# A hybrid streaming layer: TensorE in text order through attention, nine query products moved across the border between the kinds of heads, and an output half begun in score banks

## The chip, the cores and the metric

The kernel runs on one core of a Trainium2 chip. The metric is device time in microseconds (us) of one launch; the kernel before takes 1536.96 us (median of three runs, 1535.45 to 1539.69).

## The reference

One layer over 1072 rows: 32 sample rows (they also see a cache of 512 past rows), 16 learned meta rows and 1024 prompt rows, width 1024.

- RMSNorm, then one input projection into a query latent (384), a key/value latent (256), a shared rotary key (32), and query, key, value of eight "FoX" heads of 64, with a log forget value for each head.
- Heads 0 to 7 (latent heads): query from the normalised query latent (64 plain and 32 rotary columns each), key and value from the key/value latent; a mask by chunks of 64 rows.
- Heads 8 to 15 (FoX heads): causal, with the difference of cumulated log forget values added to the logits.
- Softmax, times value; both groups concatenated, one output projection (1024 x 1024), residual.
- RMSNorm, SwiGLU feed-forward (width 2816), residual, final RMSNorm.

All of it is float32: each operand is held as a rounded high part and a low part, and a product is three matmuls (high x high, high x low, low x high).

## The kernel before, in words

**Stages.** Input projection (to some 233 us of the span), attention head by head (to some 689 us), then the part called C: second half of the output projection and the feed-forward (to the end). Heads run in the order 8 to 15, then 0 to 7.

**One head.** The rows are nine query tiles (`QT`, L37): tile 0 of 48 rows, tiles 1 to 8 of 128. `attention` (L725) takes the tiles in two groups, first (5, 6, 7, 8), then (1, 2, 3, 4) with (0). For each tile, `scores` (L560) multiplies query by key into a score buffer `psS` (two buffers of two PSUM banks; tile 8 also takes one of the two `psT` banks), DVE finds the row maximum (L592) and ACT does the exponential (L597). Between the scores the loop steps a generator `state["pend"]`: the value work (`values`, L619) of the group before. A step transposes one block of probabilities on TensorE into a `psT` bank (L651, L627), ACT and DVE split it (L67, L68), and the value matmuls (L667, L668, L665, L637) of the block two steps back (`LAG`) are issued into the single bank `po`. When a group's last value matmul is done, `out` copies half of `po` on ACT (L675) and adds the halves on DVE (L678); only then may the next group write `po`. After each second head, `finish_pair` (L684) adds three steps that divide by the row sums (L706 on TensorE, L712, L713, L715).

**Fillers.** After each score tile and each step, `fill()` may draw from a second generator; it draws `rate` units a call. During heads 8 to 15 it is `latent_heads` (L445): 16 key products, 26 value products, then 18 query products (six weight blocks in the order 4, 5, 0, 1, 2, 3, three column chunks each; blocks 4 and 5 are the rotary parts). The query products read the query latent, which is loaded (L61, tiles `A_hi`, `A_lo`) into the memory that the key/value latent leaves. Their results pass through a ring of six small buffers (`room`) on their way to DRAM. At head 15 the loop empties this filler, and then `masks()` loads the shared mask operand B3 (tile `room`, from `sKR` and `sM`) into two places of the same ring; the third matmul of each score of heads 0 to 7 reads B3 (`psS<-room,x`). In heads 0 to 7 the filler is `out_half` (L537): 24 products of the FoX half of the output projection, in two half products each, with tile `psF`.

**What sets the order.** The framework's scheduler orders each engine's instructions, TensorE's too, by the text's order and by its own forecast of when operands are ready. On the chip each queue then runs in that order. SyncE (SP) issues all loads, GpSimd (POOL) the stores to DRAM.

**Border to part C.** After the last head the remaining value steps are run. The pools of attention close, and part C opens `psG` (six banks) for its products. It takes the output products of the latent half (`units`, L835) in groups of four, k = 0 to 2 of all four first and then k = 3, since the pair of heads 6 and 7 is row 3 of `A_hi` and `A_lo`; the matmuls are L845 to L847.

Of the kernel before, what the change touches and what calls it, by code (L numbers as in the profile page):

```python
# [9 lines left out]
F32 = mybir.dt.float32  # L10
# [32 lines left out]
RING = 6  # L43
# [6 lines left out]
def trunk(ctx: ExitStack, tc: tile.TileContext, a):  # L50
# [392 lines left out]
    mixed = {}  # L443

    def latent_heads():  # L445
# [24 lines left out]
        ws = [weights(*todo[0])]  # L470
        yield
        for m in range(6):
            if m + 1 < 6:
                ws.append(weights(*todo[m + 1]))
            w = ws[m]
            if m < 4:
                for c0, n in KC:
                    ps = psF.tile([128, 512], F32, tag="psF", name="psF")
                    mm3(ps[:, :n], lambda k: w[0][:, k], lambda k: w[1][:, k],
                        lambda k: l_hi[:, k, c0:c0 + n], lambda k: l_lo[:, k, c0:c0 + n], 2)  # L480
                    spill(es, sK[m, :, :, c0:c0 + n], ps[:, :n], n)
                    yield
            else:
                for k0, n in [(128 * i, 128) for i in range(4)] + [(PAST + t0, n) for t0, n in QT]:
                    ps = psF.tile([128, 512], F32, tag="psF", name="psF")
                    for k in range(2):
                        s_hi, s_lo = l_hi[:, k, k0:k0 + 128], l_lo[:, k, k0:k0 + 128]
                        pe.matmul(ps[:, :256], s_hi, w[0][:, k], start=(k == 0), stop=False)
                        pe.matmul(ps[:, :256], s_hi, w[1][:, k], start=False, stop=False)
                        pe.matmul(ps[:, :256], s_lo, w[0][:, k], start=False, stop=(k == 1))  # L490
                    spill_v(None, k0, 4 * (m - 4), ps[:n, :256], n, part()[:, :512].rearrange("p (h d) -> p h d", h=4))
                    yield
# [9 lines left out]
        ws = [weights("w_uq", order[0], 3, 128)]  # L502
        yield
        for i, m in enumerate(order):
            if i + 1 < 6:
                ws.append(weights("w_uq", order[i + 1], 3, 128))
            w = ws[i]
            for cs, (c0, n) in zip(trig, CC):
                ps = psF.tile([128, 512], F32, tag="psF", name="psF")
# [4 lines left out]
                else:  # L514
# [8 lines left out]
                    if turn[0] == RING:  # L523
                        turn[0] = 3
                yield

# [10 lines left out]
    def out_half():  # L537
# [4 lines left out]
        for m in range(8):  # L542
            out_weights(m + 2)
            w = w_ring[m]
            for c0, n in CC:
# [4 lines left out]
                for k in range(4):  # L550
# [3 lines left out]
                    if k == 1:  # L554
                        yield
                dve.tensor_tensor(out=xt[:, :n], in0=ps[:, :n], in1=xt[:, :n], op=ALU.add)
                put(sX2[128 * m:128 * m + 128, c0:c0 + n], xt[:, :n])
                yield

# [162 lines left out]

    state = {"pend": iter(()), "n": 0}

    def attention(hs, filler, steps, last):  # L725
        rate, owed = steps / (25.0 * (len(hs) - 0.7)), [0.0]

        def fill():
            if last and h == hs[0] and grps[0][0] == 5:
                return  # L730
            owed[0] += rate
            while owed[0] >= 1:
                next(filler, None)
                owed[0] -= 1

        rs = raw = None
        for h in hs:
# [14 lines left out]
            for grps in (((5, 6, 7, 8),), ((1, 2, 3, 4), (0,))):  # L752
                todo = [i for g in grps for i in g]
                P, done = {}, 0
                for j, i in enumerate(todo):
# [15 lines left out]
                state["pend"] = chain(*gens)  # L771
        for _ in filler:
            pass

# [11 lines left out]

    attention(range(8, 16), latent_heads(), 62, False)
    mixed["A"] = (slot("A_hi"), slot("A_lo"))

    attention(range(0, 8), out_half(), 48, True)  # L790
    for _ in state["pend"]:
        pass
    B.close()
    hpx.close()


    with ExitStack() as C:
# [34 lines left out]
        big = [tuple(rows4(t) for t in mixed[g]) for g in ("A", "B")]  # L832
        m_hi, m_lo = big[0]
        W = None
        units = [(m, c) for m in range(8) for c in FC]  # L835
        for u0 in range(0, len(units), 4):
            part = []
            for m, (c0, n) in units[u0:u0 + 4]:
                out_weights(8 + m + 2)
                part.append((m, c0, n, psG.tile([128, 512], F32, tag="psG", name="psG"), w_ring[8 + m]))  # L840

            for ks in ((0, 1, 2), (3,)):
                for m, c0, n, ps, w in part:
                    for k in ks:
                        pe.matmul(ps[:, :n], w[0][:, k], m_hi[:, k, c0:c0 + n], start=(k == 0), stop=False)  # L845
                        pe.matmul(ps[:, :n], w[0][:, k], m_lo[:, k, c0:c0 + n], start=False, stop=False)
                        pe.matmul(ps[:, :n], w[1][:, k], m_hi[:, k, c0:c0 + n], start=False, stop=(k == 3))  # L847
            if u0 == 12:
# [16 lines left out]
        def gate_up(W, c0, n, ah, al, between=None):  # L865
# [3 lines left out]
            def product(j):  # L869
                ps = psG.tile([128, 512], F32, tag="psG", name="psG")  # L870
                marks[2] = mm3(ps[:, :n], lambda k: gh[:, j, k], lambda k: gl[:, j, k], lambda k: big[k // 4][0][:, k % 4, cs], lambda k: big[k // 4][1][:, k % 4, cs], 8)
                return ps
# [20 lines left out]
        def down(parts, c0, n, norm=False, then=None):  # L893
            cs = slice(c0, c0 + n)
            for m in range(8):
                ps = psG.tile([128, 512], F32, tag="psG", name="psD")
                down_mm(ps[:, :n], m, cs, parts, True, True)
# [25 lines left out]
        def down_final(prev, cur, c0, n):  # L923

            cs = slice(c0, c0 + n)
            pairs = [psG.tile([128, 512], F32, tag="psG", name="psD").rearrange("p (a b) -> p a b", a=2) for _ in range(4)]
            for part in (prev, cur):
# [161 lines left out]
```

## Time and profile before

| | us |
|---|---|
| Median of three runs | 1536.96 |
| Profiled execution, its time | 1537.25 |
| Its span, first to last instruction | 1535.5 |
| TensorE (PE) busy | 1493.0 |
| VectorE (DVE) busy | 971.5 |
| ScalarE (ACT) busy | 591.4 |

PE is TensorE's matmuls, PEld its weight loads, which run beside the matmuls. A busy PE is not PE at its peak, since a matmul's shown duration covers the pipeline too. Granted clock is the share of TensorE's full clock that the chip gave. Between the span and the time of the execution lie 1.75 us.

### The profile page before, as it was taken

The numbers are of one execution on the slowest core, as the hardware profiler recorded it, in microseconds if no ns is written. First come the engines' busy times: TensorE is split into PE (matmuls) and PEld (weight loads), VectorE is DVE, ScalarE is ACT, GpSimd is POOL, SyncE is SP. The second block draws the span as 40 slices with busy tenths as digits, with TensorE's granted clock in tenths as the row PEclk, the third lists the DMA queues.
The fourth block names the chain that finished last, engine by engine and source line by source line (L and its number), as shares of the span: only waits on it lengthen the run. The fifth ranks groups of instructions, "written<-read, shape, count | busy, mean of one in ns | idle before, by whom it ended". The sixth has DMA issues, their size and how long they took to land.

```text
span 1535.5 us, 24295 instructions
## 1 busy us (share of the span) xinstructions
PE 1493.0 (97%) x9317; PEld 1433.5 (93%) x9317; DVE 971.5 (63%) x1861; ACT 591.4 (39%) x1198; POOL 198.5 (13%) x331
## 2 busy tenths in 40 slices
PE   9999998999898999989999999999999999999996
PEld 8999997888787898979999999999999999999996
DVE  8874626787966776766855655555555555655547
ACT  7443436777655666654511111111111121111124
POOL 0343242422131211200000000000000000000001
PEclk9999999999999999999999999999999999999999
DMA  6689567778587686515111111111111111111003
GB/s 196 233 258 299 172 210 249 238 218 262 147 238 185 174 212 161 148 41 206 34 50 44 54 42 42 42 42 42 42 42 42 53 58 53 44 42 42 28 1 115
DMA packets 87636, 184.19 MB, mean 120 GB/s; under 512 B 9754, under 2 KB 52954, under 8 KB 87428
## 3 DMA queue, kind: packets, MB, share of 16 engines
q1 hardware_dynamic: 70592, 128.34, 28.8%
q0 software_dynamic: 16928, 54.29, 10.1%
q8 instruction: 74, 1.21, 0.3%
q14 instruction: 42, 0.34, 0.1%
HBM read 123.93 MB, written 58.67 MB: 119 GB/s over the span
## 4 chain that ended last, share of the span: by engine, by line
PE 88%; DVE 4%; ACT 3%; issue 2%; DMA 1%; POOL 1%; DVEq 0%; SPq 0%; POOLq 0%; ACTq 0%
PE psG L122 11%; PE psG L121 11%; PE psG L123 11%; PE psD L890 5%; PE psD L891 5%; PE psD L889 5%; PE psS L589 5%; PE psT L651 4%; PE psA L123 3%; PE psA L121 3%; PE psA L122 3%; PE po L667 2%; PE po L668 2%; PE psA L386 1%; PE psA L387 1%
## 5 line engine op out<-in xcount | busy, mean ns | idle before, releaser
L898 DVE TENSOR_TENSOR x<-psD,x 128x408 f32<-128x408 f32 (+1 forms) x496 | 236.2, 522 | 4.3 <-PE psD L891 4.3
L122 PE MATMUL psG<-B_lo,gh 128*128 128x408 f32 (+1 forms) x528 | 172.8, 327 | 0.0
L121 PE MATMUL psG<-B_hi,gh 128*128 128x408 f32 (+1 forms) x528 | 172.8, 327 | 0.0
L122 PE MATMUL psG<-A_lo,gh 128*128 128x408 f32 (+1 forms) x528 | 172.6, 327 | 0.0
L121 PE MATMUL psG<-A_hi,gh 128*128 128x408 f32 (+1 forms) x528 | 172.3, 326 | 0.0
L891 PE MATMUL psD<-ah,dl 128*128 128x408 f32 (+1 forms) x528 | 172.1, 326 | 0.0
L123 PE MATMUL psG<-B_hi,gl 128*128 128x408 f32 (+1 forms) x528 | 171.8, 325 | 0.0
L123 PE MATMUL psG<-A_hi,gl 128*128 128x408 f32 (+1 forms) x528 | 171.8, 325 | 0.0
L890 PE MATMUL psD<-al,dh 128*128 128x408 f32 (+1 forms) x528 | 171.7, 325 | 0.0
L889 PE MATMUL psD<-ah,dh 128*128 128x408 f32 (+1 forms) x528 | 170.9, 325 | 0.5 <-ACT ah L67 0.5
L878 ACT ACTIVATE sl<-sl 128x408 f32<-128x408 f32 (+1 forms) x66 | 33.1, 503 | 351.3 <-DVE sl L877 351.2
L882 DVE TENSOR_TENSOR sq<-psG,rb 128x408 f32<-128x408 f32 (+1 forms) x66 | 35.0, 530 | 156.5 <-PE psG L123 156.5
L68 DVE TENSOR_TENSOR ptl<-psT,pth 128x512 fp32r<-128x512 f32 x192 | 104.6, 552 | 28.7 <-ACT pth L67 26.6
L592 DVE TENSOR_REDUCE nm<-psS 128x1 f32<-128x656 f32 (+2 forms) x144 | 104.0, 724 | 27.2 <-PE psS L589 25.6
L67 ACT ACTIVATE pth<-psT 128x512 fp32r<-128x512 f32 (+4 forms) x208 | 99.2, 480 | 55.7 <-PE psT L651 46.5
L830 POOL TENSOR_TENSOR acc<-acc,sq 128x408 f32<-128x408 f32 x10 | 10.8, 1076 | 812.4 <-ACT sq L829 811.9
L877 DVE TENSOR_TENSOR sl<-psG,rb 128x408 f32<-128x408 f32 (+1 forms) x66 | 34.9, 530 | 123.0 <-PE psG L123 123.0
L67 ACT ACTIVATE ah<-sl 128x408 fp32r<-128x408 f32 (+1 forms) x66 | 33.2, 503 | 197.2 <-DVE sl L883 125.8
L589 PE MATMUL psS<-b,a 128*128 128x328 f32 (+4 forms) x360 | 99.9, 331 | 7.4 <-ACT pb L597 6.1
L889 PEld LDWEIGHTS psD<-ah,dh 128*128 128x128 f32 x528 | 99.2, 188 | 0.9 <-ACT ah L67 0.7
L122 PEld LDWEIGHTS psG<-B_lo,gh 128*128 128x128 f32 x528 | 99.2, 188 | 0.5 <-issue 0.3
L121 PEld LDWEIGHTS psG<-B_hi,gh 128*128 128x128 f32 x528 | 99.2, 188 | 0.5 <-issue 0.2
(274 smaller groups left out, 3803.5 us busy)
## 6 DMA issues: line engine op xcount, KB each, us to landing
sg<-w_gu SPq DMA_DIRECT2D x44, 512.0 KB
a<-sQ SPq DMA_DIRECT2D x56, 268.0 KB
b<-sK SPq DMA_DIRECT2D x32, 396.0 KB
sg<-w_down SPq DMA_DIRECT2D x22, 512.0 KB
v<-sV SPq DMA_DIRECT2D x16, 512.0 KB
wst<-w_in SPq DMA_DIRECT2D x13, 512.0 KB
sV<-vt POOLq DMA_DIRECT2D x24, 256.0 KB, 4.5
sK<-room POOLq DMA_DIRECT2D x14, 396.0 KB, 4.9
```

The costliest lines, as they stand in the source:

```text
L67: first = act.activation(hi, src, AF.Copy)
L68: return first.ins, eng.tensor_tensor(out=lo, in0=src, in1=f32(hi), op=ALU.subtract).ins
L121: pe.matmul(ps, whi(k), rhi(k), start=(k == 0), stop=False)
L122: pe.matmul(ps, whi(k), rlo(k), start=False, stop=False)
L123: last = pe.matmul(ps, wlo(k), rhi(k), start=False, stop=(k == K - 1))
L589: pe.matmul(out, qa[:K, t0:t0 + nq], kb[:K, k0 + c:k0 + c + w], start=(j == 0), stop=last)
L592: dve.tensor_reduce(out=nm[:nq, j:j + 1], in_=src, axis=AX.XY if len(src.shape) == 3 else AX.X, op=ALU.max, negate=True)
L651: pe.transpose(out=pt[:, 128 * g:128 * g + 128], in_=tiles[g][1][:, c:c + 128], identity=ident)
L889: pe.matmul(ps, dh[:, m], ah[:, cs], start=first and j == 0, stop=False)
L890: pe.matmul(ps, dh[:, m], al[:, cs], start=False, stop=False)
L891: pe.matmul(ps, dl[:, m], ah[:, cs], start=False, stop=last and j == len(parts) - 1)
L898: dve.tensor_tensor(out=x2[:, m, cs], in0=ps[:, :n], in1=x2[:, m, cs], op=ALU.add)
```

## The change

- The score buffers `psS` outlive attention.
- From head 8 to the end of attention TensorE runs in the order of the text (`tc.manual_schedule`); the other engines are still ordered by the scheduler.
- `latent_heads` yields the units that a draw costs. Before the query products it idles three draws in place of one, and the query latent is loaded in three chunks of columns. After nine query products (blocks 4, 5, 0) it marks `keys`; from there on its results keep off the two ring places of B3, so `masks()` can load B3 at head 15's start. The nine products of blocks 1, 2, 3 are drawn at 0.25 a call in head 15 and in the first group of head 0; what is left of them is drawn before head 1's second group.
- `out_half` follows in the same chain of fillers. Rates change from 62 and 48 steps over 7.3 heads to 59 over 7.3 and 50 over 7.75.
- `begin()` runs k = 0 to 2 of the first four output products of the latent half, into the four banks of two score buffers, one step of three matmuls after each of the nine value steps left, and three steps behind them.
- Part C uses these four banks and two of `psG` in rotation (`bank()`), in place of six of `psG`.

```diff
-    psS = B.enter_context(tc.tile_pool(name="psS", bufs=2, space=PSUM))
+    psS = ctx.enter_context(tc.tile_pool(name="psS", bufs=2, space=PSUM))
...
             turn[0] = (turn[0] + 1) % (RING + 1)
+            if state["keys"] and turn[0] in (RING - 2, RING - 1):
+                turn[0] = RING
...
-        move(c_hi, sCQ[:, :, 0].rearrange("k p t -> p k t"))
-        move(c_lo, sCQ[:, :, 1].rearrange("k p t -> p k t"))
+        for c0, n in CC:
+            for j, t in enumerate((c_hi, c_lo)):
+                move(t[:, :, c0:c0 + n], sCQ[:, :, j, c0:c0 + n].rearrange("k p t -> p k t"))
...
-        yield
+
+        for _ in range(3):
+            yield 1
         for i, m in enumerate(order):
...
+            if i == 3:
+
+                state["keys"] = True
+                yield 0
...
+        state["made"] = True
+        yield 0
...
-        rate, owed = steps / (25.0 * (len(hs) - 0.7)), [0.0]
+        rate, owed = steps / (25.0 * (len(hs) - (0.25 if last else 0.7))), [0.0]
         def fill():
-            if last and h == hs[0] and grps[0][0] == 5:
-                return
-            owed[0] += rate
+
+            border = h == 15 or (last and h == hs[0] and len(grps) == 1)
+            owed[0] += 0.25 if border else rate
             while owed[0] >= 1:
-                next(filler, None)
-                owed[0] -= 1
+                if last and border and state["made"]:
+                    return
+                owed[0] -= next(filler, 1)
...
-            if h == hs[-1]:
-                for _ in filler:
-                    pass
-                if not last:
-                    masks()
+            if h == hs[-1] and not last:
+                while not state["keys"]:
+                    next(filler)
+                masks()
...
+                if last and h == hs[1] and len(grps) == 2:
+                    while not state["made"]:
+                        next(filler)
+                    mixed["A"] = (slot("A_hi"), slot("A_lo"))
...
-    attention(range(8, 16), latent_heads(), 62, False)
-    mixed["A"] = (slot("A_hi"), slot("A_lo"))
-
-    attention(range(0, 8), out_half(), 48, True)
+    first = latent_heads()
+
+    order_pe = ctx2.enter_context(ExitStack())
+    order_pe.enter_context(tc.manual_schedule(engines={mybir.EngineType.PE}))
+    attention(range(8, 16), first, 59, False)
+
+    attention(range(0, 8), chain(first, out_half()), 50, True)
...
+    def begin():
+        for u in (0, 2):
+            out_weights(10)
+            pair = psS.tile([128, 2, 512], F32, tag="psS", name="psS")
+            for j in range(2):
+                early.append(pair[:, j])
+                for k in range(3):
+                    out_products(units[u + j], pair[:, j], (k,))
+                    yield
+
+    begun = begin()
     for _ in state["pend"]:
+        next(begun, None)
+    for _ in begun:
         pass
+    order_pe.close()
...
-        psG = C.enter_context(tc.tile_pool(name="psG", bufs=6, space=PSUM))
+        psG = C.enter_context(tc.tile_pool(name="psG", bufs=2, space=PSUM))
...
+        drawn = [4]
+
+        def bank():
+
+            t = drawn[0] % 6
+            drawn[0] += 1
+            return early[t] if t < 4 else psG.tile([128, 512], F32, tag="psG", name="psG")
```

## Rows read from the trace of the kernel before

**Rows 1.** The page: span, then busy time, share and instructions of each engine.
```profile
span 1535.5 us, 24295 instructions
PE 1493.0 (97%) x9317; PEld 1433.5 (93%) x9317; DVE 971.5 (63%) x1861; ACT 591.4 (39%) x1198; POOL 198.5 (13%) x331
```

**Rows 2.** Busy time by stretches of attention: length, engines, granted clock, DMA share, GB/s.
```profile
220.00:260.00 40.00, 35.73 (x242) 31.04 (x241) 19.18 (x35) 21.00 (x51) 12.81 (x23) 1.00 0.63 216
260.00:360.00 100.00, 98.03 (x680) 86.90 (x678) 79.50 (x162) 75.48 (x188) 34.23 (x61) 1.00 0.75 225
360.00:380.00 20.00, 19.03 (x132) 16.18 (x131) 16.14 (x33) 16.65 (x43) 3.40 (x6) 1.00 1.01 315
380.00:400.00 20.00, 17.94 (x118) 14.84 (x116) 16.11 (x31) 12.59 (x31) 3.21 (x8) 1.00 0.93 219
400.00:420.00 20.00, 18.22 (x102) 15.16 (x101) 19.07 (x40) 11.72 (x28) 5.81 (x8) 0.92 0.39 125
420.00:440.00 20.00, 16.69 (x106) 15.09 (x107) 15.70 (x31) 13.00 (x32) 6.20 (x9) 1.00 0.62 177
440.00:460.00 20.00, 19.53 (x123) 17.44 (x122) 11.24 (x23) 11.46 (x28) 8.55 (x15) 1.00 0.96 275
460.00:480.00 20.00, 15.65 (x92) 13.43 (x91) 10.99 (x22) 10.16 (x25) 4.20 (x8) 0.96 0.86 215
480.00:660.00 180.00, 176.67 (x1148) 161.77 (x1147) 126.38 (x238) 111.85 (x264) 37.58 (x66) 0.99 0.64 167
```

**Rows 3.** The same view: head 14, and the end of attention.
```profile
381.00:412.00 31.00, 27.56 (x164) 22.65 (x163) 27.18 (x52) 19.61 (x48) 7.08 (x13) 0.94 0.75 186
660.00:676.00 16.00, 14.51 (x96) 12.49 (x95) 12.37 (x26) 11.96 (x31) 0.00 (x0) 1.00 0.08 27
676.00:689.00 13.00, 8.80 (x54) 6.74 (x53) 9.33 (x20) 6.73 (x16) 1.84 (x6) 0.91 0.03 8
689.00:699.20 10.20, 10.20 (x49) 10.08 (x50) 1.72 (x5) 0.67 (x2) 0.00 (x0) 0.78 1.00 399
```

**Rows 4.** TensorE in order of time at the border: start, us, line, idle before.
```profile
411.77 0.49 PE L589 MATMUL psS<-b,a 128*128 128x328 f32 x2
...
424.31 0.31 PE L589 MATMUL psS<-x,a 70*128 70x328 f32 x1
...
469.01 0.43 PE L551 MATMUL psF<-B_hi,woh 128*128 128x358 f32 x1 [1.25 <-ACT B_hi L713]
...
469.89 0.32 PE L589 MATMUL psS<-room,x 106*128 106x328 f32 x1
```

**Rows 5.** SyncE's queue in order of time: start of the issue, us of it.
```profile
369.13 0.38 SPq L61 DMA_DIRECT2D A_hi<-sCQ  x1
373.86 0.38 SPq L61 DMA_DIRECT2D A_lo<-sCQ  x1
...
383.11 0.41 SPq L58 DMA_DIRECT2D wst<-w_uq  x1
...
459.40 1.24 SPq L61 DMA_DIRECT2D room<-sKR  x3
```

**Rows 6.** TensorE: a tile 3 score of head 8, the first key product, the first query product.
```profile
241.81 0.43 PE L589 MATMUL psS<-b,a 128*128 128x400 f32 x1
...
245.62 0.45 PE L121 MATMUL psF<-A_hi,woh 128*128 128x396 f32 x1 [0.78 <-ACT woh L67]
...
387.67 0.41 PE L121 MATMUL psF<-A_hi,woh 128*128 128x358 f32 x1
```

**Rows 7.** TensorE, one turn of the value bank in head 2: last write, next group's first.
```profile
527.31 0.48 PE L665 MATMUL po<-ptm,v 128*128 128x512 f32 x1
...
529.41 0.65 PE L637 MATMUL po<-pth,v 112*128 112x96 f32 x4
```

**Rows 8.** TensorE after attention: first output matmul, and the first with k = 3.
```profile
688.81 0.68 PE L845 MATMUL psG<-A_hi,woh 128*128 128x408 f32 x1 [1.10 <-DVE raw L712]
...
697.10 0.34 PE L845 MATMUL psG<-A_hi,woh 128*128 128x408 f32 x1
```

More of the change, by code (lines that the diff above doesn't have):

```diff
@@ L443, in trunk @@
     mixed = {}
+    state = {"pend": iter(()), "n": 0, "keys": False, "made": False}
     def latent_heads():
@@ L481, in latent_heads @@
                     spill(es, sK[m, :, :, c0:c0 + n], ps[:, :n], n)
-                    yield
+                    yield 1
             else:
@@ L491, in latent_heads @@
                     spill_v(None, k0, 4 * (m - 4), ps[:n, :256], n, part()[:, :512].rearrange("p (h d) -> p h d", h=4))
-                    yield
+                    yield 1
         hi, lo = slot("A_hi"), slot("A_lo")
         c_hi, c_lo = (t[:, :3 * T].rearrange("p (k t) -> p k t", k=3) for t in (hi, lo))
-        move(c_hi, sCQ[:, :, 0].rearrange("k p t -> p k t"))
-        move(c_lo, sCQ[:, :, 1].rearrange("k p t -> p k t"))
+        for c0, n in CC:
+            for j, t in enumerate((c_hi, c_lo)):
+                move(t[:, :, c0:c0 + n], sCQ[:, :, j, c0:c0 + n].rearrange("k p t -> p k t"))
         trig = [f32(ring[i][:, :716].rearrange("p (j t) -> p j t", j=2)) for i in range(3)]
@@ L502, in latent_heads @@
         ws = [weights("w_uq", order[0], 3, 128)]
-        yield
+        for _ in range(3):
+            yield 1
         for i, m in enumerate(order):
@@ L524, in latent_heads @@
                         turn[0] = 3
-                yield
+                yield 1
+        state["made"] = True
+        yield 0
     w_ring, w_next = [], [0]
@@ L554, in out_half @@
                     if k == 1:
-                        yield
+                        yield 1
                 dve.tensor_tensor(out=xt[:, :n], in0=ps[:, :n], in1=xt[:, :n], op=ALU.add)
                 put(sX2[128 * m:128 * m + 128, c0:c0 + n], xt[:, :n])
-                yield
+                yield 1
     def scores(h, ops, i, rs):
@@ L771, in attention @@
                 state["pend"] = chain(*gens)
-        for _ in filler:
-            pass
+        if last:
+            for _ in filler:
+                pass
     mixed["B"] = (slot("B_hi"), slot("B_lo"))
@@ L785, in masks, with out_products @@
         mixed["B3"] = B3
-    attention(range(8, 16), latent_heads(), 62, False)
-    mixed["A"] = (slot("A_hi"), slot("A_lo"))
-    attention(range(0, 8), out_half(), 48, True)
+    first = latent_heads()
[3 more added lines that the diff above has]
+    attention(range(0, 8), chain(first, out_half()), 50, True)
+    units = [(m, c) for m in range(8) for c in FC]
+    def out_products(unit, ps, ks):
+        (m, (c0, n)), w = unit, w_ring[8 + unit[0]]
+        for k in ks:
+            for j, (wj, t) in enumerate(((0, 0), (0, 1), (1, 0))):
+                pe.matmul(ps[:, :n], w[wj][:, k], rows4(mixed["A"][t])[:, k, c0:c0 + n], start=(k == 0 and j == 0), stop=(k == 3 and j == 2))
+    early = []
+    def begin():
[8 more added lines that the diff above has]
+    begun = begin()
     for _ in state["pend"]:
+        next(begun, None)
+    for _ in begun:
         pass
+    order_pe.close()
     B.close()
@@ L832, in trunk @@
         big = [tuple(rows4(t) for t in mixed[g]) for g in ("A", "B")]
-        m_hi, m_lo = big[0]
         W = None
-        units = [(m, c) for m in range(8) for c in FC]
         for u0 in range(0, len(units), 4):
@@ L839, in trunk @@
                 out_weights(8 + m + 2)
[L840 to L847, printed above, removed]
+                part.append((m, c0, n, early[len(part)] if u0 == 0 else bank(), w_ring[8 + m]))
+            for ks in ((3,),) if u0 == 0 else ((0, 1, 2), (3,)):
+                for j, (m, c0, n, ps, w) in enumerate(part):
+                    out_products(units[u0 + j], ps, ks)
             if u0 == 12:
@@ L869, in product @@
             def product(j):
-                ps = psG.tile([128, 512], F32, tag="psG", name="psG")
+                ps = bank()
                 marks[2] = mm3(ps[:, :n], lambda k: gh[:, j, k], lambda k: gl[:, j, k], lambda k: big[k // 4][0][:, k % 4, cs], lambda k: big[k // 4][1][:, k % 4, cs], 8)
@@ L895, in down @@
             for m in range(8):
-                ps = psG.tile([128, 512], F32, tag="psG", name="psD")
+                ps = bank()
                 down_mm(ps[:, :n], m, cs, parts, True, True)
@@ L925, in down_final @@
             cs = slice(c0, c0 + n)
-            pairs = [psG.tile([128, 512], F32, tag="psG", name="psD").rearrange("p (a b) -> p a b", a=2) for _ in range(4)]
+            pairs = [bank().rearrange("p (a b) -> p a b", a=2) for _ in range(4)]
             for part in (prev, cur):
```

1 line of the change is left out of this document (removed).

## The prediction

> **What bounds the kernel now.** I read the page first: PE is busy for 1493.0 of 1535.5 us [rows 1], so it is the bound nearly everywhere, and a PE change counts only where PE waits or is slowed. The page can't say where that is, since a busy PE isn't PE at its peak. So I read busy time by stretches next, and take weight loads (PEld) as the measure, since each matmul has one. In heads 1 to 6, the stretch 480 to 660, PE idles for 3.33 us in 180 and PEld is busy for 161.77: 0.899 of the time [rows 2]. That is the pace at which PE goes through this mix of work with next to no wait. A stretch with less PEld is worth PEld / 0.899 at that pace, and the rest of it is lost:
>
> - 220 to 260: 31.04 / 0.899 = 34.5 of 40, lost 5.5. Head 8 starts without value work of a head before.
> - 360 to 380: lost 2.0; 380 to 440: (14.84 + 15.16 + 15.09) / 0.899 = 50.2 of 60, lost 9.8; 440 to 460: lost 0.6; 460 to 480: 13.43 / 0.899 = 14.9, lost 5.1 [rows 2].
> - 660 to 676: 12.49 / 0.899 = 13.9 of 16, lost 2.1 [rows 3]. 676 to 689: PE is busy for 8.80 of 13; right behind, 689 to 699.2, it is full but at a granted clock of 0.78, that is partly at 1.2 GHz [rows 3].
>
> (Loads take longer at the lower clock, so the losses are if anything a little larger.) The border between the FoX heads and the latent heads and the end of attention together hold some 25 us. Everything behind 700 us runs on PE without gaps and keeps its instructions.
>
> Last, the order of time shows what PE does in those stretches. Head 15's first key matmuls are issued at 411.77, and the other operand of the same score only at 424.31 [rows 4]. In between stand query products: DVE and ACT have no score to work on. And the first matmul with B3 is at 469.89 [rows 4], 10.5 us after SP issues the B3 load at 459.40 [rows 5], which had to wait for the ring that the query products use; the matmul before the wait itself starts late at 469.01.
>
> **The change, part by part.** The sum is against the profiled execution, 1537.25 us (span 1535.5 and 1.75 around it); the median of the runs is 0.29 below that. Plus is time saved.
>
> *B3 loaded before head 15.* No matmul is added or taken away; nine products' results just go round B3's places. The load then has all of head 15, some 30 us, in place of 10.5. Of the 5.1 lost in 460 to 480 I take 4: the first scores of head 0 still feed a softmax that has to start. Bounds 0 and 5.1. **+4**
>
> *Nine query products spread over head 15 and head 0's first group.* Head 15 has 24 calls of `fill`, head 0's first group 13: at 0.25 a call 6 and 3.25 products, all nine. The draws before them fit: heads 8 to 14 have 171 calls, at 59 / 182.5 a call 55.3 units, and up to `keys` there are 1 + 16 + 26 + 3 + 9 = 55. So head 15's start drains nothing in a lump, and scores are no longer issued in two halves 12.5 us apart. What this can give back is the 9.8 lost in 380 to 440. Against all of it stands DVE: in head 14 it is busy for 27.18 of 31 us [rows 3], since the rotary work of blocks 4 and 5 lies there, and those six products stay in head 14. Bounds 0 and 9.8; I take **+6**, as the DVE-bound head 14 is the first half of it. The 2.0 of 360 to 380 stay, since PE has no filler there in either order.
>
> *The first query product in the queue.* In order, PE stops at it until query latent and weights are in, and all scores and value steps behind it stop too, and with them DVE and ACT. Now the product comes 18.5 us after the latent's place is free (369.13 to 387.67 [rows 5, 6]). In the text it comes four draws later, 4 / 0.323 = 12.4 calls; head 13 has 24 calls in some 20 us, so 10.3 us. Without any help it would wait 8.2 us. Loading by chunks needs a third of the bytes first, but the low half still waits in SP's queue until 373.86, and the weights, behind trigonometric tables and the next head's values in the same queue, until 383.11 [rows 5]. Bounds 0 and 8.2; I take **-3**: bytes ahead of the weights fall, and the scheduler that orders SP sees PE's order.
>
> *The start.* By the text the first key product follows six score tiles and one value step of head 8: at some 241.8, where tile 3's score now starts. It can't run before 245.62, when its weights are split [rows 6]. Now other work fills these 3.8 us; in order they are idle, though later work is then readier. Bounds 0 and 3.8. **-2.5**
>
> *Last head.* The rate 50 / 193.75 = 0.258 spreads 48 half products over 191 calls in heads 0 to 7 and so leaves some to head 7's last scores. Of the 2.1 lost in 660 to 676 I take **+1.5**.
>
> *Output half begun in the score banks.* Its 36 matmuls now stand from 688.81 to 697.10 [rows 8]: 8.3 us, the first 5 us at half clock. They move up between the nine value steps of the tail, 676 to 689, where PE is busy for 8.80 of 13 us, and so they find 4.2 us of idle and lengthen the tail by some of their rest. I let the k = 3 matmuls, which need the last division's result, start at 690.5 in place of 697.10. Bounds: 2 if the 36 matmuls merely delay the tail's own chain and save just their clock, 8.3 if they vanish. **+6.6**. Nothing late takes its place: the DMA share in 689 to 699.2 is 1.00 [rows 3], that is the residual's loads, and they start when attention's last head has been read, as before; the first is far ahead of the first sum. The rotation of six banks gives part C as many as before: 0.
>
> *Text order in the steady heads.* Now 180 us hold 3.33 us of idle [rows 2], because the scheduler puts filler into waits. In the text fillers come at every fourth call wherever that is. The dearest wait is the turn of the one `po` bank: from the last write of a group to the first of the next 2.10 us pass (527.31 to 529.41 [rows 7]), now filled with half a product and transposes; a head has three such turns. Bounds per head: 0 (the text has a score tile between the two writes), and 2.1 (one turn of three with nothing in it). I take 0.25 a head more than now, as the idle row is measured with practically the same sequence of scores and steps, and only the fillers' places differ: 16 heads, **-4**.
>
> Here a rule speaks against the change. The row: in 420 to 440 PE is busy for only 16.69 of 20 us, in many short waits, and the granted clock stays 1.00 [rows 2]. The Trainium skill, "TensorE: Matmul & The Clock Gate", section "A second HAM failure mode: psum-queue depth-cycling", says that short idles between groups of matmuls that cycle through PSUM banks can send the clock back and forth between its levels. By the row more short waits cost just themselves; by that page each could cost a stretch at 1.2 GHz too, and this is the last rival below.
>
> Sum: 4 + 6 - 3 - 2.5 + 1.5 + 6.6 - 4 = 8.6; 1537.25 - 8.6 = 1528.7, **1529 us**.
>
> **The rivals.**
>
> *The waits of text order eat it all (slower).* PE in order stands at the `po` turn wherever the text has only a transpose between the writes. One turn in three short by half of its 2.10 us, and as much again at tile 8, which holds one of the two `psT` banks until its exponential is done, make 2.1 us a head less the idle that is there already (0.5): 1.6 x 16 = 26; the `po` turns alone 1.05 x 16 = 16.8. The rest of the sum is +12.6, so it decides from 12.6 / 16 = 0.79 us a head. With 16.8: 1537.25 - 12.6 + 16.8 = 1541.5; with 26: 1551. For it: the 3.33 us of idle are so few because fillers stand just there. Against it: a PE that falls behind lets DVE (126.38 of 180 busy [rows 2]) and ACT catch up. I put it at 1543.
>
> *The border is DVE's.* If head 14's DVE load sets the pace, spreading products gives nothing: the +6 goes, 1535. For it 27.18 of 31 [rows 3]; against it DVE's 10.99 and 11.24 of 20 in the last two stretches [rows 2].
>
> *Nothing is lost in order.* All of 9.8, 5.1, 2.1 and 6.6 comes back and the three costs are 0: 23.6 saved, 1514. For it, that text and present order differ so little in 480 to 660.
>
> *The clock.* One drop a head, each as dear as that in 400 to 420 (0.92 there, so 1.6 us lost [rows 2]), costs 25.6: 1554. Against it the granted 1.00 in 420 to 440.
>
> **How the numbers follow.** Forecast 0.47, with its own range 1520 to 1534; text-order waits 0.23; nothing lost 0.15; DVE's border 0.12; clock 0.03. A measurement of this kernel tells about 0.3% from no change, 4.6 us: below 1532.4 is faster, above 1541.6 slower. Faster: 0.36 of the forecast and 0.15, together 0.51. Same: 0.11 of the forecast, 0.10 of DVE's border, 0.02 of the waits: 0.23. Slower: 0.21 of the waits, 0.02, 0.03: 0.26. The range takes in the waits of 1543 with some more and nearly the whole of "nothing lost": 1513 to 1546, with the 26 us case and the clock left out.
>
> **What would show it.** Right: B3's load issued near head 15's start, and head 0's first `psS<-room,x` with its other operands; each head's six score matmuls unbroken; PEld's share in the 100 us ahead of head 1 near 0.88; the first output matmul some 12 us before attention's end, k = 3 right behind it, the granted clock there 1.00. Wrong: PE waits "po <- raw L678" of over 0.8 us a head in heads 1 to 6; a long wait of the first query or key product; a stretch behind 700 us that has grown; or the clock falling in the steady heads.

## The result, and the profile after

The changed kernel takes 1611.92 us (median of 4 runs, 1609.34 to 1614.42) against 1537.24 for the kernel before beside it: ratio 1.048, 95% interval 1.0457 to 1.0503. It is 75 us slower where 8 us less was forecast, and outside the range. The profiled execution took 1611.3 us, its span 1609.5.

The page after, answering [rows 1]: span, busy time, share and instructions. The work is the same; PE's share is 94% in place of 97%, so about 46 us more of it are idle (88.7 in place of 42.5), and PE's busy time has grown by 28 us.

```profile
span 1609.5 us, 24258 instructions
PE 1520.8 (94%) x9317; PEld 1445.4 (90%) x9317; DVE 982.5 (61%) x1861; ACT 591.2 (37%) x1198; POOL 198.5 (12%) x331
```

Where it went is read by stage, from the order of matmuls in both traces. Attention starts at 233 us in both. The last output product starts at 738.1 us before and at 786.2 after: **48 us** are lost by then. From there to the last matmul it takes 786.6 us before and 812.7 after: **26 us** in the feed-forward, where the change was costed at nothing.

Busy time by stretches after, against [rows 2] (length, then PE, PEld, DVE, ACT, POOL, granted clock, DMA share, GB/s):

```profile
220.00:260.00 40.00, 33.47 (x215) 29.51 (x214) 15.42 (x28) 17.93 (x43) 10.84 (x20) 0.87 0.53 185
400.00:420.00 20.00, 15.08 (x97) 13.25 (x95) 13.66 (x25) 12.04 (x27) 1.53 (x6) 0.93 1.06 315
420.00:440.00 20.00, 16.46 (x78) 15.31 (x79) 15.20 (x36) 9.23 (x23) 7.34 (x11) 0.71 0.60 173
480.00:660.00 180.00, 162.89 (x1037) 150.12 (x1036) 117.16 (x220) 103.68 (x247) 37.41 (x65) 0.97 0.66 171
```

In the steady heads PE now idles for 17.1 us in 180, not 3.33, and 1036 weight loads fit where 1147 did. The clock, 0.99 there before, is 0.97, and at the border it falls to 0.71. What PE stands at is in its waits over the whole span (line, what it waited for: us in total, times, longest):

```profile
PE po L649 <- DVE raw L690: 15.7, 15, 1.5
PE po L679 <- DVE raw L690: 15.1, 15, 2.1
PE psT L639 <- DVE ptm L668: 6.0, 6, 1.5
PE psT L718 <- ACT pb L609: 5.0, 4, 1.5
PE psS L121 <- DVE sl L923: 4.9, 2, 3.2
PE psF L121 <- ACT room L527: 4.3, 1, 4.3
PE psF L121 <- ACT woh L67: 3.5, 1, 3.5
PE psS L121 <- DVE x L944: 3.3, 20, 0.2
```

The two waits at `po` make 30.8 us in 30 turns; before they were 2.6 us. The `psS L121` rows lie in the feed-forward, at the score banks that part C now draws.

One turn of `po` in head 0, from the group (5, 6, 7, 8) to (1, 2, 3, 4), in order of time (start, us, engine, line; rows of weight loads and queues left out). The old group's last write starts at 518.80. `po` comes free only with VectorE's addition at 520.35. That is late for two reasons: ScalarE's copy of half of `po` ends only at 520.24, and in VectorE's own queue the maximum of a score tile (0.97 us) and a split (0.55 us) are ahead of the addition. In text order PE has two transposes to do in that time, and then it stands for 1.59 us in front of the next group.

```profile
518.80 0.48 PE L677 MATMUL po<-ptm,v 128*128 128x512 f32 x1
518.92 0.97 DVE L604 TENSOR_REDUCE nm<-psS 128x1 f32<-128x784 f32 x1
519.12 0.38 PE L663 MATMUL psT<-ident,pa 128*128 128x128 f32 x2
...
519.65 0.59 ACT L687 ACTIVATE half<-po 64x512 f32<-64x512 f32 x1
519.80 0.55 DVE L68 TENSOR_TENSOR ptl<-psT,pth 128x384 fp32r<-128x384 f32 x1
...
520.35 0.68 DVE L690 TENSOR_TENSOR raw<-po,half 64x512 f32<-64x512 f32 x1
...
521.09 0.50 PE L679 MATMUL po<-pth,v 128*128 128x512 f32 x1 [1.59 <-DVE raw L690]
```

The same turn in the kernel before ([rows 7] shows another, from (1, 2, 3, 4) to tile 0):

```profile
493.15 0.48 PE L665 MATMUL po<-ptm,v 128*128 128x512 f32 x1
...
494.71 0.68 DVE L678 TENSOR_TENSOR raw<-po,half 64x512 f32<-64x512 f32 x1
...
495.45 0.50 PE L667 MATMUL po<-pth,v 128*128 128x512 f32 x1
```

The turn itself is no longer after than before: 2.29 us from write to write against 2.30, and the addition starts 1.55 and 1.56 us after the last write. Before, PE did two transposes, the six matmuls of a score tile and three matmuls of an output product in it; in text order it has the transposes alone.

### The profile page after: what moved, and what is told of

It reads as the page before. It is cut to its first block, busy times and chain, and to the rows that moved or that the text cites. A ratio compares the mean times of both kernels' runs of the same rounds, so it can differ in the third digit from the quotient of the medians.

```text
span 1609.5 us, 24258 instructions
## 1 busy us (share of the span) xinstructions
PE 1520.8 (94%) x9317; PEld 1445.4 (90%) x9317; DVE 982.5 (61%) x1861; ACT 591.2 (37%) x1198; POOL 198.5 (12%) x331
## 4 chain that ended last, share of the span: by engine, by line
PE 82%; DVE 8%; ACT 5%; issue 3%; DMA 2%; POOL 0%; DVEq 0%; SPq 0%; ACTq 0%
PE psS L121 7%; PE psS L122 7%; PE psS L123 7%; PE psS L601 5%; PE psG L121 4%; PE psS L935 4%; PE psG L123 4%; PE psG L122 4%; PE psT L663 4%; PE psS L937 3%; PE psS L936 3%; PE psA L121 3%; PE psA L123 3%; PE psA L122 3%; PE po L679 2%
## 5 line engine op out<-in xcount | busy, mean ns | idle before, releaser
L944 DVE TENSOR_TENSOR x<-psS,x 128x408 f32<-128x408 f32 (+1 forms) x330 | 172.1, 541 | 39.1 <-PE psS L937 38.1
L121 PE MATMUL psS<-A_hi,gh 128*128 128x408 f32 (+1 forms) x360 | 118.8, 330 | 8.1 <-DVE sl L923 4.9
L935 PE MATMUL psS<-ah,dh 128*128 128x408 f32 (+1 forms) x348 | 119.9, 345 | 1.7 <-DVE x L944 1.7
L936 PE MATMUL psS<-al,dh 128*128 128x408 f32 (+1 forms) x348 | 115.2, 331 | 0.0
L937 PE MATMUL psS<-ah,dl 128*128 128x408 f32 (+1 forms) x348 | 115.0, 331 | 0.0
L122 PE MATMUL psS<-B_lo,gh 128*128 128x408 f32 (+1 forms) x360 | 114.6, 318 | 0.0
L121 PE MATMUL psS<-B_hi,gh 128*128 128x408 f32 (+1 forms) x360 | 114.3, 317 | 0.0
L122 PE MATMUL psS<-A_lo,gh 128*128 128x408 f32 (+1 forms) x360 | 113.9, 316 | 0.0
L123 PE MATMUL psS<-A_hi,gl 128*128 128x408 f32 (+1 forms) x360 | 113.8, 316 | 0.0
L123 PE MATMUL psS<-B_hi,gl 128*128 128x408 f32 (+1 forms) x360 | 113.7, 316 | 0.0
L121 PEld LDWEIGHTS psS<-A_hi,gh 128*128 128x128 f32 x360 | 67.5, 187 | 19.4 <-DVE x L944 7.3
```

Of the source, the lines that this page charges most:

```text
L121: pe.matmul(ps, whi(k), rhi(k), start=(k == 0), stop=False)
L122: pe.matmul(ps, whi(k), rlo(k), start=False, stop=False)
L123: last = pe.matmul(ps, wlo(k), rhi(k), start=False, stop=(k == K - 1))
L935: pe.matmul(ps, dh[:, m], ah[:, cs], start=first and j == 0, stop=False)
L936: pe.matmul(ps, dh[:, m], al[:, cs], start=False, stop=False)
L937: pe.matmul(ps, dl[:, m], ah[:, cs], start=False, stop=last and j == len(parts) - 1)
```

## Experiments

The theory after the two traces: text order makes PE stand at waits that the scheduler had filled (the 48 us), and the turn of part C's banks, four of which are now halves of two pair tiles, makes the 26 us. The rivals: the border edit or the score banks cost the attention; the feed-forward is late for another reason. All ratios are against runs of the kernel before on the same chip.

**Text order alone**, on the kernel before:

```diff
+    order_pe = ctx2.enter_context(ExitStack())
+    order_pe.enter_context(tc.manual_schedule(engines={mybir.EngineType.PE}))
     attention(range(8, 16), latent_heads(), 62, False)
...
+    order_pe.close()
     B.close()
```

> The kernel before with one edit: TensorE keeps the order of the text through attention; fillers, banks and part C stay as they were. Theory A (the text order costs the attention stage: TensorE stands 31 us in its queue at po behind VectorE's add into raw, 6 us at psT behind ptm, and the clock falls in the gaps): the first output product comes 40 to 60 us later than 688.8 us, the feed-forward keeps its 786.6 us, and the time is 1577 to 1600 us. Rival B (the text order is harmless, the products moved across the border and the two score banks kept for part C cost the time): first output product within 10 us of 688.8, time 1530 to 1547 us. Rival C (text order alone is worse than in the changed kernel, because the lump of query products at the border is now waited for in order): over 1600 us.

1612.32 us, ratio 1.0496 (1.047 to 1.0522): +74 us, rival C. The first output product comes at 764.8 us instead of 688.8, and the feed-forward keeps its 786.6 us. From the last value product of tiles 1 to 4 in head 12 to that in head 13 it takes 50.2 us, against 35.5 in the changed kernel and 22.3 before. From 397.5 to 500 us PE waits for 14.0 us at `psF`; in the next run but one, with text order and the border edit, for 4.3 in the same heads (393 to 470 us). So the lump at the border is waited for in order, and the border edit is worth much, but only once text order is there.

**The changed kernel without text order** (the line above is left out of it):

> The changed kernel without its text order; the products across the border, the output half begun in score banks and part C's drawing of banks all stay. Theory A (text order makes the attention's loss, the banks of part C the feed-forward's 26 us): the waits at po fall under 5 us in sum, the output projection ends at 735 to 750 us instead of 786.2, the feed-forward still takes about 812 us, and the time is 1550 to 1566 us. Rival B (border and banks cost the attention, not the order): the output projection ends after 770 us and the time is over 1590 us. Rival D (the feed-forward's 26 us follow from the late end of attention, not from the banks): feed-forward back at 787 us, time 1524 to 1540 us.

1559.12 us, ratio 1.0139 (1.0123 to 1.0154). Theory A: the waits at `po`, counted as the 30.8 above, fall to 2.2 us (1.2 and 1.0), the feed-forward stays at 815.2, and the last output product starts at 732.2 us, 3 us earlier than that theory said. Text order costs 52.8 us in the changed kernel.

**Part C's banks as before**, text order and border kept, no output product begun early:

```diff
-    psS = ctx.enter_context(tc.tile_pool(name="psS", bufs=2, space=PSUM))
+    psS = B.enter_context(tc.tile_pool(name="psS", bufs=2, space=PSUM))
...
-        psG = C.enter_context(tc.tile_pool(name="psG", bufs=2, space=PSUM))
+        psG = C.enter_context(tc.tile_pool(name="psG", bufs=6, space=PSUM))
```

> The changed kernel with text order and border, but with part C's six single banks from one pool as before, and no output product begun in score banks. Theory A (the drawing of banks costs the feed-forward 26 us): feed-forward 785 to 790 us, attention as late as in the changed kernel, time 1584 to 1594 us; what the begun output half had hidden comes back in it. Rival D (the feed-forward's 26 us have another cause): feed-forward at 810 us or more, time 1608 to 1622 us.

1586.31 us, ratio 1.0317 (1.0299 to 1.0334). The feed-forward is back at 786.6 us, attention nearly as late as in the changed kernel (last value product at 738.1; there it is 741.0, with output products begun in between). Theory A.

**Pair banks alone**, on the kernel before: `bank()` as in the change, over two pair tiles and two single ones.

> The kernel before with one edit: part C draws its six banks in a fixed turn, four of them as halves of two pair tiles and two from a pool of two; nothing is begun early, and attention is untouched. Theory A (the turn or the pair tiles cost 26 us in the feed-forward): feed-forward 805 to 815 us, time 1556 to 1566 us, with TensorE standing at pair banks only. Rival D (no effect by themselves): time 1534 to 1541 us. Rival E (only part of the 26 us is the banks' and the rest the order of the work that the scheduler makes around them): 1543 to 1554 us.

1561.45 us, ratio 1.0154 (1.0139 to 1.017), feed-forward 814.1 us: theory A again, and the 23 us don't need a late attention. It is pairs or their fixed turn, and the next run parts the two.

**Six single banks in the same fixed turn**, on the kernel before:

```diff
-        psG = C.enter_context(tc.tile_pool(name="psG", bufs=6, space=PSUM))
+        psG = C.enter_context(tc.tile_pool(name="psG", bufs=1, space=PSUM))
+        six = [psG.tile([128, 512], F32, tag=f"psG{i}", ...) for i in range(6)]
...
+            return six[t]
```

> The kernel before with one edit: part C draws its six banks in the same fixed turn as the run with pairs, but each bank is a tile of its own. Theory P (a pair tile makes TensorE's next product in one half wait for VectorE's or ScalarE's reading of the other half): no waits at the banks, feed-forward 785 to 789 us, time 1534 to 1542 us. Rival F (it is the fixed turn that costs, since a bank still being read comes up while another is free): feed-forward 800 to 815 us, time 1550 to 1564 us.

1537.25 us, ratio 0.9995 (0.9986 to 1.0004): no cost. It is the pairs. The same stretch in the kernel before, with pairs, and with single banks in turn:

```profile
800.00:1500.00 700.00, 700.00 (x4256) 698.71 (x4255) 392.32 (x761) 124.48 (x184) 5.34 (x5) 1.00 0.13 43
```
```profile
800.00:1500.00 700.00, 696.90 (x4156) 676.86 (x4155) 392.22 (x744) 115.42 (x172) 0.00 (x0) 1.00 0.13 43
```
```profile
800.00:1500.00 700.00, 700.00 (x4255) 698.70 (x4254) 392.56 (x761) 124.36 (x183) 5.34 (x5) 1.00 0.13 43
```

With pairs PE is still "busy" for 99.6% of the stretch; what shows the loss is the count, 4156 matmuls in place of 4256, and PEld's busy time. Waits that the profile lists stand at weight loads, between 800 and 1550 us in the run with pairs; the three rows make 13.2 of the 27.5 us (814.1 less 786.6):

```profile
PEld psP L121 <- DVE x L910: 7.0, 19, 0.4
PEld psP L121 <- DVE sl L889: 3.8, 1, 3.8
PEld psP L901 <- DVE x L910: 2.4, 3, 1.2
```

**Pairs, with a pair's halves three draws apart** (the edit against the run with pairs):

```diff
-            return early[t] if t < 4 else psG.tile(...)
+            return psG.tile(...) if t % 3 == 2 else early[(0, 2, 0, 1, 3)[t]]
```

> The kernel before with part C's six banks as in the run with pairs, drawn in another turn: first half of one pair, first half of the other, a single bank, then the second halves in the same way and the other single bank, so that a pair's two halves are three draws apart and not one. Theory H (a product into one half waits until the other half, drawn just before it, has been read out): the waits at pair banks go nearly away, feed-forward 785 to 795 us, time 1536 to 1546 us. Rival G (any view of a pair tile waits more, whatever the turn): feed-forward about 814 us, time 1555 to 1565 us.

1545.61 us, ratio 1.0052 (1.0035 to 1.0069), feed-forward 798.9 us. The order of the draws alone takes back 15 of the 27 us. So a product waits for the half next to its own, and less so when that half was drawn longer ago. Theory H's time came, its feed-forward of 785 to 795 us didn't: 12 us stay, of which 3.5 are listed as 19 waits of at most 0.2 us at pair halves. What the rest is stays open. A row of 800 to 1500 in it:

```profile
800.00:1500.00 700.00, 700.00 (x4204) 688.07 (x4203) 392.11 (x750) 119.15 (x178) 0.00 (x0) 1.00 0.13 43
```

By these runs the wait hangs on how the program holds the banks, two as one tile, and not on the banks themselves. The Trainium skill, "PSUM — Partial Sum Buffer", section "PSUM bank collisions raise a hardware error", forbids two engines one bank and quadrant at once, and says that different banks run clean. The run with six single banks agrees: there, PE writes one bank while VectorE reads its neighbour, at no cost.

**The border edit alone**: the changed kernel in the scheduler's order and with part C's banks as before.

> The changed kernel with the order of before on TensorE and part C's banks as before: what is left of the change is the fillers alone, nine query products across the border and their rates, and B3's earlier loading. Theory A (the border edit was worth something, about what the two kernels with text order show, 26 us, but most of that was the lump's cost in text order only): time 1527 to 1537 us, with the first query product no longer waited for. Rival N (under the scheduler's order the lump was already hidden): 1535 to 1541 us.

1536.30 us against 1537.49, ratio 0.9988 (0.9978 to 0.9998). The ranges of both theories take that in; the gain of 1.2 us is hardly clear of no change, and the profiled executions show none (1537.21 and 1537.25), so rival N fits better. The edit does what it says, and it is given back later. The border and the steady heads, first before, then in this run:

```profile
380.00:480.00 100.00, 88.04 (x534) 75.95 (x533) 73.11 (x143) 58.94 (x141) 27.96 (x46) 0.98 0.75 202
```
```profile
380.00:480.00 100.00, 91.39 (x557) 79.15 (x557) 75.12 (x151) 62.18 (x150) 26.91 (x45) 0.97 0.82 228
480.00:660.00 180.00, 172.68 (x1121) 157.68 (x1120) 123.12 (x234) 110.29 (x263) 37.63 (x65) 1.00 0.64 165
```

The border holds 3.2 us more of weight loads, and 480 to 660 4.1 us fewer than [rows 2]; PE idles there for 7.3 us in place of 3.33. Counted by the last value product of tiles 1 to 4, head 15 ends 3.8 us earlier than before, and head 7 1.0 us later. The moved query products push the output half back: its products run from 489.7 to 672.8 us, before from 463.0 to 657.7. That the steady heads miss just these fillers has not been tried.

**Border and begun output half, with single banks throughout**: the scheduler's order, and the score pairs given back after the first four output products.

```diff
+            if u0 == 4:
+                SC.close()
+                psH.append(... tile_pool(name="psH", bufs=4, space=PSUM, side="right"))
...
-            return early[t] if t < 4 else psG.tile(...)
+            return (psH[0] if t < 4 else psG).tile(...)
```

> The changed kernel without text order, and with the score pairs given back after the first four output products: part C then draws six banks that are tiles of their own. So the border and the output half begun in score banks both stay, and both suspected costs are gone. Theory P and A together: output projection ends at 730 to 738 us, feed-forward 785 to 789 us, time 1528 to 1539 us; the begun half is worth 0 to 6 us against the run with the border alone. Rival F (the turn costs, pair or not): feed-forward over 800 us, time over 1550 us.

1530.48 us, ratio 0.9947 (0.9934 to 0.996), feed-forward 786.6: faster than both kernels, and 5.8 us below the border alone. The tail of attention, against [rows 3], keeps its clock:

```profile
676.00:689.00 13.00, 11.82 (x77) 10.26 (x75) 8.27 (x17) 5.40 (x14) 1.84 (x6) 1.00 0.08 18
689.00:699.20 10.20, 10.15 (x60) 10.16 (x61) 4.81 (x11) 4.02 (x9) 0.00 (x0) 1.00 1.02 414
```

**What in text order costs.** First, an edit meant to let both engines read out `po` side by side:

```diff
+            if idx != [0]:
+                dve.tensor_copy(row, po[0:64, :n])
+                dve.tensor_tensor(out=row, in0=row, in1=half[:, :n], op=ALU.add)
+                return
```

> The changed kernel with one edit: VectorE copies po's upper half into raw beside ScalarE's copy of the lower half, and adds the two from SBUF, so that po is handed back one addition earlier, at the price of one more VectorE instruction for each of 31 groups. Theory A (TensorE stands at po because its next product into po comes straight behind the old one's reading out, in order): the waits at po fall from 31 us to 10 to 20 us and the time to 1594 to 1604 us. Rival V (VectorE is the bound in these heads, so that its extra instruction takes back what po gives): waits at po fall, waits at psS and psT rise, time 1608 to 1618 us.

1619.41 us, ratio 1.0528 (1.0514 to 1.0542): worse by 7.5, and the waits at `po` haven't moved, against both expectations:

```profile
PE po L649 <- DVE raw L691: 15.6, 15, 1.5
PE po L679 <- DVE raw L691: 15.0, 15, 2.1
```

The edit didn't do what it was meant to. VectorE's copy no longer takes ScalarE's half, yet in none of the 32 groups does it start before ScalarE's copy out of the same bank has ended, and in 19 it starts within 0.05 us of that end. In this turn VectorE had been idle for 0.46 us:

```profile
504.42 0.59 ACT L687 ACTIVATE half<-po 64x512 f32<-64x512 f32 x1
...
505.05 0.68 DVE L691 COPY raw<-po 64x512 f32<-64x512 f32 x1 [0.46 <-ACT half L687]
```

So the two reads of `po` still follow each other, and `po` comes free no earlier. The run doesn't price the turn. The next edit goes at its other end: the first product into `po` one step later. In two runs it moved nothing (the mark was set and cleared in one call):

> The changed kernel with one edit to its text: the first product into po of a group is written one step later (behind the next step's scores and transposes), so that in text order other work of TensorE stands between the old po's reading out and the new po. Theory A (the loss is TensorE standing in its queue at a wait that the text puts too near its releaser, the po turn above all): the waits at po fall from 31 us to under 12 us, the output projection ends 15 to 30 us earlier than 786.2 us, time 1582 to 1598 us. Rival W (the wait is only handed on, because ScalarE and VectorE are behind in text order anyway): po's waits fall but those at psT and psS rise by as much, time 1606 to 1616 us.

1612.97 us, that is a repeat of the changed kernel.

> The run with single banks throughout, with text order put back and the first product into po one step later. Theory A: 1587 us (that run's 1530.5 and the 48 to 50 us that text order costs, less the 26 us of the pairs that it doesn't have) less what the later po gives in the run beside it, so 1556 to 1574 us; above 1530.5 because the waits at psT and psF and the slower clock stay. Rival W: 1580 to 1590 us.

1584.59 us, ratio 1.0298 (1.0283 to 1.0313): the single-bank run in plain text order. Text order costs 54.1 us there, as against 52.8 with pairs and 50.0 with the old banks (1586.31 against 1536.30). Then the edit as meant (`held` is set in `out()`, and the product held back is written behind the next step's transposes):

```diff
+    def behind(keep, turn=False):
+        h = held[0] if turn else 0
+        if turn:
+            held[0] = 0
-        while len(queue) > keep:
+        while len(queue) > keep + h:
             queue.pop(0)()
...
+            held[0] = 1
...
+                behind(LAG)
...
-                behind(LAG)
+                behind(LAG, True)
```

> The changed kernel with the first product into po of each group really moved one step later in TensorE's text (in the earlier run of that name the edit had moved nothing: the mark was set and cleared in one call, so that run is a repeat of the changed kernel). Theory A (a wait that the text puts too near its releaser is a stall, and distance takes it away): waits at po fall from 31 us to under 15 us, time 1585 to 1603 us. Rival W (it is only handed on, to psT, psS or the next product): the same po waits or as much at other banks, time 1606 to 1616 us.

1588.76 us, ratio 1.0334 (1.0318 to 1.035): 23 us come back by writing one product a step later. Its waits:

```profile
PE po L653 <- DVE raw L696: 9.5, 8, 1.5
PE psT L642 <- DVE ptm L673: 5.7, 6, 1.5
...
PE psT L724 <- ACT pb L609: 3.8, 3, 1.5
PE psT L667 <- DVE ptl L68: 3.6, 8, 0.8
...
PE po L684 <- DVE raw L696: 2.1, 6, 0.5
```

The `po` waits fall from 30.8 to 11.6 us, the others hardly rise. Theory A; and with single banks:

> The run with single banks throughout, with text order and with that later first product into po; the same without it took 1584.6 us. Theory A: 1557 to 1575 us, by as much below 1584.6 as the run beside it stands below the changed kernel. Rival W: 1579 to 1590 us.

1560.92 us, ratio 1.0159 (1.0143 to 1.0174): 23.7 less than without it. 30.4 us above the scheduler's order stay. Up to the last value product it is 31.8 us: 24.2 more of gaps between matmuls, in waits at `psT`, `psF` and the rest of `po`, and 7.6 of matmuls that took longer. These were not taken apart further. Under the scheduler's order the edit is worth nothing:

> The run with single banks throughout (1530.5 us), in the scheduler's order, with the later first product into po. Theory A (the scheduler already puts other work at the turn, 1.2 us of waits at po in its trace): 1527 to 1534 us, no difference to be seen. Rival: the scheduler takes its due times from the text and gains from the distance, 1518 to 1526 us.

1531.24 us, ratio 0.9961 (0.9949 to 0.9974), against 1530.48 and 0.9947 without it.

**Text order in the steady heads only**, from head 1 on, in the single-bank kernel:

> The run with single banks throughout, with text order for TensorE from head 1 of the second attention half on (heads 1 to 7 and the begun output half), the scheduler's order before that. Theory A (every steady head loses 2 to 6 us to text order; from the end of head 0 to the end of head 7 the run with old banks took 207.0 us in text order and the one with the border alone 185.3 us): 1548 to 1556 us. Rival L (the loss is made at the border, by the query products and head 15's queue, and the steady heads are only late by it): 1528 to 1538 us.

1563.13 us, ratio 1.0162 (1.0145 to 1.0179). Rival L falls: from head 0's last value product of tiles 1 to 4 to head 7's it takes 209.9 us, against 184.9 in the scheduler's order, 3.6 us a head. The time is above both ranges, since head 0 takes 45.5 us instead of 40.1. Its value products of tiles 1 to 4 are stepped between head 1's scores, and so stand behind the switch in the text; there PE stands in front of the first output product, which comes at 484.98 us, until its weights are split. In the scheduler's order that product comes at 488.17, after other work, with a wait of 0.2 us.

```profile
PE psF L564 <- ACT woh L67: 3.1, 1, 3.1
```

## Why the prediction was wrong

The path from the kernel before goes through the runs: 1537.5, border -1.2, begun output half in single banks -5.8, pair banks +28.6, text order +52.8: 1611.9. By the steps of the forecast:

- **What bounds the kernel.** PE, rightly, and 25 us lost at the border and the end, rightly seen. Wrong was to take the 3.33 idle us of the steady heads for a property of the sequence of scores and steps. It was the scheduler's.
- **B3 (+4), nine query products (+6), last head (+1.5).** The mechanism came: in the run with the border alone B3's load is issued 26.3 us before its first matmul (434.41 and 460.72). The three, 11.5 in sum, gave 1.2. At the border PE got 3.2 / 0.899 = 3.6 us back; then the pace at which heads 0 to 6 were taken to run on fell, with 7.3 us of idle in 180 instead of 3.33. So what was won early couldn't be added up as if the later heads kept their pace. With text order the same edit is worth 26 us (1612.32 against 1586.31), since there the lump is waited for.
- **The first query product (-3).** No wait of 0.2 us or more before it. 4.3 us of wait come two products later, at `psF`'s turn behind the rotary work of the product before (the `ACT room L527` row). The size was about right by luck, the place was wrong.
- **The start (-2.5).** 3.5 us of wait at the first key product; head 8 ends 6.9 us later in all, and the granted clock, which the sum leaves out, is 0.87 in 220 to 260 and was 1.00 before.
- **Output half in the score banks (+6.6).** 5.8 measured. The step that failed there is the sentence that the rotation of six banks gives part C as many as before, 0: the same number, but two tiles of two banks. It cost 23 to 29 us.
- **Text order in the steady heads (-4).** This step failed most. Measured: 25 us in seven heads, and 50 to 54 us in attention as a whole. The sign named beforehand, over 0.8 us of `po` waits a head, came: 8.4 us between 480 and 660, some six heads. "Practically the same sequence of scores and steps" was the error: the fillers' places are what fills the waits, and the lower bound of 0 rested on a score tile between the two writes that, in the turn shown, the scheduler had put there and the text doesn't have. The rival of text-order waits had the mechanism and its place, the turn of `po`, and put 16.8 us on it at one turn in three; it was 30 turns of 48 at 1.03 us, and with the waits at `psT` and the clock text order cost about three times the 16.8.
- **The clock.** As a rival it was given 0.03. From 233 us to the last value product, text order makes 50.1 us of difference (738.1 against 688.0, same border and banks); the gaps between matmuls, summed from both traces, are 65.0 and 26.2 us, so 38.8 of it are idle and 11.3 are matmuls that took longer. In the changed kernel the granted clock is 0.71 in 420 to 440, behind the 4.3 us gap that ends at 420.04, so a part of that stretch ran at 1.2 GHz. It falls behind shorter waits too: in 303 to 313 us of the run with the old banks, with two waits of 1.47 us at `psT` and `po`, it is 0.83, and 1.00 in the run with the border alone; up to the last value product it falls ten times in the one and three times in the other. By the Trainium skill, "TensorE: Matmul & The Clock Gate", section "A second HAM failure mode: psum-queue depth-cycling", short idles between groups can cost that; the runs agree, and here the slower matmuls are somewhat over a fifth of the 50.1 us.

## What to carry to other kernels

Before an engine is bound to the text, walk its text past each buffer that there is only one of. Between the last write of the old contents and the first of the new the text has to hold as much work as reading them out takes, or the engine stands; here a product moved one step later gave 23 us back. Idle that a scheduler leaves at 2% says nothing about the text beneath it. And count tiles, not banks: here the halves of a two-bank tile, drawn one after the other, waited for each other's reading, and six tiles of one bank didn't.

## What was not expected of the hardware

A loss of 27.5 us in the feed-forward's 786.6 hid in a PE that reads 99.6% busy: 4156 matmuls in 700 us against 4256, and the commonest of the waits listed, 19 times, is of at most 0.4 us. The number of instructions in a fixed stretch showed it, and PEld's busy time; PE's did not. And VectorE's reading out of a bank stayed behind ScalarE's reading of the same bank when it no longer took ScalarE's result: 505.05 us against an end at 505.01, with VectorE idle before. Whether the two can read one bank side by side no run here shows.
